# One 32 KB row per load, six buffers and two load queues in a row-wise infinity norm

## The chip, the cores and the metric

The kernel runs on one core of a Trainium2 chip. The metric is the device time of one execution in microseconds (us). The kernel before took 629.88 us, the median of three runs (629.82 to 629.88).

## The reference

The input `x` is 8192 rows by 8192 columns of float32, 268.4 MB. The output is one number per row, the largest absolute value of that row (`np.linalg.norm(x, ord=np.inf, axis=1)`), 32 KB in all. Every element is read once, and one reduction is done on it.

## The kernel before

A row of `x` is 32 KB. The 8192 rows are spread over 128 partitions, so that each partition reduces 64 rows; "row" below means one such step, 128 rows of `x`, one in each partition, 4 MB. The 64 rows form two stages.

**Bulk**, rows 0 to 47 (line 65 to 72). Each load (line 68) brings two neighbouring rows into each partition, 64 KB per partition and 8 MB in all, and one VectorE instruction (line 63, called through `absmax` at line 69) reduces both to two numbers in `r_bulk`. There are 24 such loads. Within a block of eight rows per partition the addresses of a partition are contiguous.

**Tail**, rows 48 to 63 (line 75 to 98). A buffer still holds two rows, but each row is loaded and reduced in the pieces that the list `TAIL` names (line 17 to 22): eight rows whole (8192 columns), five rows in halves of 4096, two in quarters of 2048, and the last as 2048, 2048, 2048, 1024, 512, 512. A piece's maximum goes into a cell of `part`, and one reduction of `part` gives `r_tail` for rows 48 to 62. The last row's first five maxima are put right behind that row's data in its own buffer, so that its last piece and those five numbers are reduced together, over 517 columns, into `r_fin`.

Buffers: the pool `sbuf` has three of 64 KB per partition (line 51). A load into a buffer waits until the reduction that read it three buffers earlier has ended; apart from that, and from a wait for the landing of the load that used the same completion semaphore before (there are eight in turn), loads are issued as fast as the queue takes them.

Queues: all loads of `x` go through one queue, SyncE's (SP below), in the order in which they are written. `r_bulk` is stored through ScalarE's queue (ACT, line 73) after the last bulk reduction, `r_tail` through the same (line 88), `r_fin` through SP at the end (line 99). VectorE does all reductions, in the order of the rows. ScalarE and GpSimd do no arithmetic on the data.

Of the kernel before, what the change touches and what calls it, by code (L numbers as in the profile page):

```python
# [1 line left out]
logging.getLogger("concourse").setLevel(logging.ERROR)  # L3

# [1 line left out]

# [4 lines left out]

F32 = mybir.dt.float32
X = mybir.AxisListType.X

TAIL = (
    [[8192]] * 8
    + [[4096, 4096]] * 5
    + [[2048] * 4] * 2  # L20
    + [[2048, 2048, 2048, 1024, 512, 512]]
)


@with_exitstack
def kernel(
    ctx: ExitStack,
    tc: tile.TileContext,
    x: bass.AP,
    out: bass.AP,  # L30
    G: int = 4,
    B: int = 2,
    BUFS: int = 3,
):
    nc = tc.nc
    P = nc.NUM_PARTITIONS
    rows, cols = x.shape


    n_tail = len(TAIL)  # L40
    assert n_tail % B == 0
    n_bulk_rows = rows // P - n_tail
    assert n_bulk_rows % (G * B) == 0
    A = n_bulk_rows // (G * B)
    split = n_bulk_rows * P
    x_b = x[:split].rearrange("(a p n b) c -> a n p (b c)", p=P, a=A, n=G, b=B)
    out_b = out[:split].rearrange("(a p n b) -> p a (n b)", p=P, a=A, n=G, b=B)
    x_t = x[split:].rearrange("(p t b) c -> t p (b c)", p=P, b=B)
    out_t = out[split:].rearrange("(p t) -> p t", p=P)

    sbuf = ctx.enter_context(tc.tile_pool(name="sbuf", bufs=BUFS))
    outp = ctx.enter_context(tc.tile_pool(name="outp", bufs=1))

    k_last = len(TAIL[-1])
    r_bulk = outp.tile([P, A, G * B], F32)
    r_tail = outp.tile([P, n_tail], F32)
    r_fin = outp.tile([P, 1], F32)
    k_max = max(len(r) for r in TAIL[:-1])
    part = outp.tile([P, n_tail - 1, k_max], F32)
    nc.vector.memset(part[:], 0.0)  # L60

    def absmax(o, i):
        nc.vector.reduce_max(out=o, in_=i, axis=X, apply_absolute_value=True)  # L63

    for a in range(A):
        for n in range(G):
            t = sbuf.tile([P, B * cols + 16], F32, tag="t")
            nc.sync.dma_start(out=t[:, : B * cols], in_=x_b[a, n])  # L68
            absmax(
                r_bulk[:, a, n * B : (n + 1) * B],  # L70
                t[:, : B * cols].rearrange("p (b c) -> p b c", b=B),
            )
    nc.scalar.dma_start(out=out_b, in_=r_bulk[:])

    for i in range(0, n_tail, B):
        t = sbuf.tile([P, B * cols + 16], F32, tag="t")
        for j in range(B):
            r = i + j
            at = j * cols
            last = r == n_tail - 1  # L80
            for k, w in enumerate(TAIL[r]):
                nc.sync.dma_start(  # L82
                    out=t[:, at : at + w], in_=x_t[i // B][:, at : at + w]
                )
                if last and k == k_last - 1:

                    absmax(r_tail[:, : n_tail - 1], part[:])
                    nc.scalar.dma_start(
                        out=out_t[:, : n_tail - 1], in_=r_tail[:, : n_tail - 1]
                    )  # L90
                    absmax(r_fin[:], t[:, at : B * cols + k_last - 1])
                elif last:
                    absmax(
                        t[:, B * cols + k : B * cols + k + 1], t[:, at : at + w]
                    )
                else:
                    absmax(part[:, r, k : k + 1], t[:, at : at + w])
                at += w
    nc.sync.dma_start(out=out_t[:, n_tail - 1 :], in_=r_fin[:])


# [1 line left out]
_INS = ['x']  # L103
_OUTS = [((8192,), 'float32')]


# [23 lines left out]
```

## Time and profile before

| what | value |
|---|---|
| median of three runs | 629.88 us |
| the profiled execution's own time | 629.88 us |
| its span, first to last instruction | 628.1 us |
| VectorE (DVE) busy | 552.7 us, 88% |
| bytes read from HBM | 268.44 MB, 427 GB/s over the span |
| loads of two rows / of one row / of 4096, 2048, 1024, 512 columns | 24 / 8 / 10, 11, 1, 2 |
| median us from issue to landing, whole rows of the tail | 37.0 |
| `r_bulk` store, 24 KB, from issue to landing | 57.9 us |

The profile comes from one execution taken by the hardware profiler. Its span is 1.78 us shorter than that execution's time; what lies around the span is not in the trace. The profiled execution took just the median of the runs. The line of DMA busy tenths shows, for each of 40 slices of the span, how busy the core's 16 DMA engines were on average. In a timeline, "x9" after an instruction means that nine instructions of that engine followed one another without a gap and are shown merged under the first one's name; "idle before <-" says how long the engine stood still ahead of it and what ended that.

### The profile page before, as it was taken

What the parts mean: (1) busy time and instruction counts of PE and PEld (TensorE: products, weight loads), DVE (VectorE), ACT (ScalarE), POOL (GpSimd) and SP (SyncE); (2) the same over time, 40 slices, a digit from 0 to 9 for tenths busy, and PEclk for the clock granted to TensorE, in tenths of its full rate; (3) what the DMA queues carried; (4) which work ended last, traced back from release to release, by engine and by line L of the source; (5) the groups of instructions that cost most, each with busy time, mean ns of one, the idle gap of its engine ahead of it and who ended that gap; (6) DMA issues with size and microseconds to landing.
All of it is one profiled execution on the core that took longest, in us unless ns stands there. A gap on an engine that the chain in (4) does not pass through costs nothing.

```text
span 628.1 us, 196 instructions
## 1 busy us (share of the span) xinstructions
DVE 552.7 (88%) x58; POOL 0.2 (0%) x4
## 2 busy tenths in 40 slices
DVE  0588988889988889888898888998889999999998
POOL 0000000000000000000000000000000000000000
DMA  9999999999999999999999999999999999999996
GB/s 401 413 455 413 455 413 455 413 455 413 455 413 455 409 459 413 455 413 455 413 455 413 455 413 455 413 455 413 455 405 430 434 435 432 420 432 432 424 426 274
DMA packets 9138, 268.49 MB, mean 427 GB/s; under 512 B 1968, under 2 KB 1968, under 8 KB 2352
## 3 DMA queue, kind: packets, MB, share of 16 engines
q1 hardware_dynamic: 8208, 268.44, 99.1%
q10 hardware_dynamic: 928, 0.03, 0.1%
q14 instruction: 2, 0.02, 0.0%
HBM read 268.44 MB, written 0.03 MB: 427 GB/s over the span
## 4 chain that ended last, share of the span: by engine, by line
DMA 64%; DVE 30%; another core or an unknown queue 4%; issue 1%; SPq 0%
DMA t<-in_x_dram 64%; DVE r_bulk L63 23%; DVE part L63 5%; DVE t L63 1%; SPq L82 0%; DVE r_fin L63 0%; SPq L68 0%
## 5 line engine op out<-in xcount | busy, mean ns | idle before, releaser
L63 DVE TENSOR_REDUCE r_bulk<-t 128x2 f32<-128x16384 f32 x24 | 413.3, 17219 | 70.5 <-DMA t<-in_x_dram 70.5
L63 DVE TENSOR_REDUCE part<-t 128x1 f32<-128x4096 f32 (+2 forms) x26 | 130.0, 5067 | 1.3 <-DMA t<-in_x_dram 1.3
L63 DVE TENSOR_REDUCE t<-t 128x1 f32<-128x2048 f32 (+2 forms) x5 | 8.6, 1746 | 0.4 <-DMA t<-in_x_dram 0.4
L60 DVE MEMSET part<- 128x60 f32 x1 | 0.1, 108 | 0.8 <-PEq L114 0.8
L63 DVE TENSOR_REDUCE r_fin<-t 128x1 f32<-128x517 f32 x1 | 0.7, 692 | 0.0
L63 DVE TENSOR_REDUCE r_tail<-part 128x15 f32<-128x60 f32 x1 | 0.2, 216 | 0.0
L114 POOL MEMSET const-bfloat16-1.0<- 128x1 bf16 x1 | 0.1, 101 | 0.0
L114 POOL MEMSET const-uint8-127<- 128x1 uint8 x1 | 0.1, 101 | 0.0
L114 POOL MEMSET const-float32-0.0<- 128x1 f32 x1 | 0.1, 98 | 0.2 <-issue 0.2
L114 POOL MEMSET const-float32-1.0<- 128x1 f32 x1 | 0.1, 98 | 0.0
## 6 DMA issues: line engine op xcount, KB each, us to landing
t<-in_x_dram SPq DMA_DIRECT2D x8, 4096.0 KB, 37.0
t<-in_x_dram SPq DMA_DIRECT2D x10, 2048.0 KB, 30.4
t<-in_x_dram SPq DMA_DIRECT2D x11, 1024.0 KB, 24.6
t<-in_x_dram SPq DMA_DIRECT2D x1, 512.0 KB, 15.9
t<-in_x_dram SPq DMA_DIRECT2D x2, 256.0 KB, 13.2
t<-in_x_dram SPq DMA_DIRECT2D x24, 40.7
out_dram<-r_bulk ACTq DMA_DIRECT2D x1, 24.0 KB, 57.9
out_dram<-r_tail ACTq DMA_DIRECT2D x1, 7.5 KB, 5.6
```

Of the source, the lines that this page charges most:

```text
L60: nc.vector.memset(part[:], 0.0)
L63: nc.vector.reduce_max(out=o, in_=i, axis=X, apply_absolute_value=True)
L114: nc = _bacc.Bacc("TRN2", target_bir_lowering=False, num_devices=1)
```

## The change

Loads of the bulk bring one row each: 48 loads of 32 KB per partition take the place of 24 of 64 KB, and 48 reductions over 8192 columns that of 24 over 16384. The pool has six buffers of one row each in place of three of two rows, so it holds the same bytes. A tail row too has a buffer of its own. The loads, bulk and tail counted through, go in turn to SP's and ACT's queue. The `r_bulk` store moves from ACT's queue to GpSimd's (POOL) and is written into the program near the end. `TAIL`, and so the sizes of all pieces, is unchanged. In the compiled order of VectorE the reduction of `part` into `r_tail` stood ahead of the last row's pieces; now it stands between the last row's fifth piece and `r_fin`.

```diff
-    B: int = 2,
-    BUFS: int = 3,
+    G: int = 8,
+    BUFS: int = 6,
...
-    x_b = x[:split].rearrange("(a p n b) c -> a n p (b c)", p=P, a=A, n=G, b=B)
+    x_b = x[:split].rearrange("(a p n) c -> a n p c", p=P, a=A, n=G)
...
-    x_t = x[split:].rearrange("(p t b) c -> t p (b c)", p=P, b=B)
+    x_t = x[split:].rearrange("(p t) c -> t p c", p=P)
...
+    queues = (nc.sync, nc.scalar)
+    n_loads = 0
+
+    def load(o, i):
+        nonlocal n_loads
+        queues[n_loads % 2].dma_start(out=o, in_=i)
+        n_loads += 1
+
     for a in range(A):
         for n in range(G):
-            t = sbuf.tile([P, B * cols + 16], F32, tag="t")
-            nc.sync.dma_start(out=t[:, : B * cols], in_=x_b[a, n])
-            absmax(
-                r_bulk[:, a, n * B : (n + 1) * B],
-                t[:, : B * cols].rearrange("p (b c) -> p b c", b=B),
-            )
-    nc.scalar.dma_start(out=out_b, in_=r_bulk[:])
+            t = sbuf.tile([P, cols + 16], F32, tag="t")
+            load(t[:, :cols], x_b[a, n])
+            absmax(r_bulk[:, a, n : n + 1], t[:, :cols])
 
-    for i in range(0, n_tail, B):
-        t = sbuf.tile([P, B * cols + 16], F32, tag="t")
-        for j in range(B):
...
+    for r in range(n_tail):
+        t = sbuf.tile([P, cols + 16], F32, tag="t")
+        at = 0
+        last = r == n_tail - 1
+        for k, w in enumerate(TAIL[r]):
+            load(t[:, at : at + w], x_t[r][:, at : at + w])
+            if last and k == k_last - 1:
+
+                absmax(r_tail[:, : n_tail - 1], part[:])
+                nc.gpsimd.dma_start(out=out_b, in_=r_bulk[:])
+                nc.scalar.dma_start(
+                    out=out_t[:, : n_tail - 1], in_=r_tail[:, : n_tail - 1]
                 )
...
+                absmax(r_fin[:], t[:, at : cols + k_last - 1])
+            elif last:
+                absmax(t[:, cols + k : cols + k + 1], t[:, at : at + w])
+            else:
+                absmax(part[:, r, k : k + 1], t[:, at : at + w])
+            at += w
     nc.sync.dma_start(out=out_t[:, n_tail - 1 :], in_=r_fin[:])
```

## The prediction

> **What bounds the kernel now.** I read the page's rows of busy time and DMA first, then the groups by shape, then stretches of the DMA rate, and last VectorE's timeline from 440 us on.
>
> ```profile
> DVE 552.7 (88%) x58; POOL 0.2 (0%) x4
> DMA  9999999999999999999999999999999999999996
> q1 hardware_dynamic: 8208, 268.44, 99.1%
> out_dram<-r_bulk ACTq DMA_DIRECT2D x1, 24.0 KB, 57.9
> ```
>
> The DMA engines are busy in every slice: loading bounds the kernel. VectorE is not far behind: 552.7 of 628.1 us. The next lines give a stretch, its length, VectorE's busy time in it and (last two columns) the DMA share and GB/s.
>
> ```profile
> 100.00:440.00 340.00, 303.90 (x18) 0.00 (x0) 1.00 1.00 434
> 470.00:484.00 14.00, 14.00 (x1) 0.00 (x0) 1.00 1.01 433
> 519.40:542.70 23.30, 23.30 (x3) 0.00 (x0) 1.00 1.00 428
> ```
>
> The third stretch is one in which, by the list of waits, SP's queue stood 23.2 us on the `r_bulk` store's landing. The DMA share is 1.00 there too: loads issued earlier covered it. So no stretch holds a DMA pause that more buffers or a second queue could close.
>
> VectorE's timeline (start, length, instruction, idle before):
>
> ```profile
> 448.11 17.22 DVE L63 TENSOR_REDUCE r_bulk<-t 128x2 f32<-128x16384 f32 x1 [2.06 <-DMA t<-in_x_dram]
> 467.49 17.22 DVE L63 TENSOR_REDUCE r_bulk<-t 128x2 f32<-128x16384 f32 x1 [2.15 <-DMA t<-in_x_dram]
> 484.62 60.23 DVE L63 TENSOR_REDUCE part<-t 128x1 f32<-128x8192 f32 x7
> 545.24 43.37 DVE L63 TENSOR_REDUCE part<-t 128x1 f32<-128x8192 f32 x9 [0.38 <-DMA t<-in_x_dram]
> ...
> 593.97 21.96 DVE L63 TENSOR_REDUCE part<-t 128x1 f32<-128x4096 f32 x9 [0.38 <-DMA t<-in_x_dram]
> ...
> 621.01 4.01 DVE L63 TENSOR_REDUCE t<-t 128x1 f32<-128x2048 f32 x3 [0.20 <-DMA t<-in_x_dram]
> 625.05 0.69 DVE L63 TENSOR_REDUCE r_fin<-t 128x1 f32<-128x517 f32 x1
> ```
>
> This is the view that decides. The last load of two rows lands at 467.5, and VectorE gets both at once. Though rows come singly from then on, it works without a pause until 544.85: seven more rows pass before it has caught up, since a row takes it (60.23 - 8.68) / 6 = 8.59 us (8.68 is the mean of that group) and a load about 9.7. From 545.24 it follows the loads closely, and ends 625.74. So what arrives late or in lumps near the end is regained slowly.
>
> **The change part by part.** The sum is made against the profiled execution, 629.88 us, which is the median too; its 1.78 us outside the span I leave.
>
> *Two queues.* What does an engine do with two queues that both hold loads? The `r_bulk` store on ACT's queue beside loads on SP's shows it. Its 24 KB are 768 runs of 32 bytes (128 partitions by six blocks), 48 per DMA engine, and 57.9 / 48 = 1.21 us each: just the time of one 32 KB run of a load on one engine (9.7 us / 8 partitions per engine). The trace's packet records agree: on an engine 32-byte packets lie between neighbouring 32 KB packets, one or a few at each gap, so queues take turns run by run. Two loads of equal runs, one on each queue and started together, then go at half speed each and land together, one run (1.2 us) apart, every 2 x 9.7 us. Nothing pulls them apart: a buffer comes free 8.6 or 17.2 us after a landing of the pair and four rows are still queued or in flight, two per queue, so neither queue runs dry. VectorE needs 17.2 us per 19.4 us pair, so the bulk hides this. The tail does not.
>
> The rows are an even number, so rows 54 and 55 (the last whole ones) form the last full pair. Row 55 lands when it does now, at 545.24 plus s, the cost of smaller runs; row 54 lands 1.2 us before it, instead of some 9.7. From row 54's landing VectorE has: two rows, 2 x 8.59 = 17.2; ten halves at (43.37 - 8.59 - 4.41) / 7 = 4.34, 43.4; eight quarters at (21.96 - 4.34 - 2.28) / 7 = 2.19, 17.5; the last row, 2 x 2.19 + 4.01 = 8.4; `r_tail`, 0.13 (616.09 - 615.96) and `r_fin` with its gap, 0.7. Together 87.3 us. Does it ever stand still in that time? Its lag behind landings is 16 us at first (17.2 - 1.2); a pair of halves takes it 8.7 us against 9.7 of loading, a pair of quarters 4.4 against 4.9. The last row's first pair starts at 545.2 + 17.2 + 43.4 + 17.5 = 623.3 and lands about 620. It never waits: 3 us stay in hand. VectorE, not the last load, sets the end.
>
> *32 KB runs for 64 KB in the bulk (s).* Bulk starts run from 42.11 to 448.11 over 21 loads: 19.333 us, 9.667 per row. Tail rows: (545.24 - 467.49) / 8 = 9.719. The difference, 0.052 x 48 rows = 2.5 us, is an upper bound, because the store's packets lie in the tail's figure; the lower is 0 (the rates 434 and 433 hardly differ). I take s = 1.2, the middle.
>
> So `r_fin` ends at 545.24 + 1.2 - 1.2 + 87.3 = 632.5 against 625.74: +6.8 us.
>
> *48 reductions for 24.* 2 x 8.59 for 17.14 (484.62 - 467.49): nothing, and covered by 2 us of idle time per load while loads bound. *More instructions on two queues.* An issue takes 0.33 us on SP, 0.35 to 0.44 on ACT; ACT issues nothing else in the bulk, and loads are issued at least a row ahead. Nothing, unless queued loads run out. *Six buffers.* The same bytes; they remove no pause, since there is none.
>
> *`r_tail` beside `r_fin`.* Its store took 5.6 us to land, among loads; `r_fin`'s took 1.4, with none. Now it is issued 0.7 us ahead of `r_fin`'s end with loads done: between 0 and 5.6 - 0.7 - 1.4 = 3.5 us. I take 0.1, since the loads that slowed it are gone.
>
> *`r_bulk` store on POOL.* POOL waits only for row 47's reduction and has nothing queued behind the store but the end. If it too goes run by run, with two loads' runs ahead of each of its 48, it needs at most 48 x 2.4 = 116 us from some 485 us, and less once runs are halved: done by 601, 30 us before the end. Ends: 0, and, if it lands last, 1 to 4 us (from `r_fin`'s 1.4 us to `r_tail`'s 5.6 after a 1.4 that is there anyway). I take 0.
>
> Sum: 629.88 + 6.8 + 0.1 = 636.8 us.
>
> A rule against my main step: the Trainium skill, "DMA: Bandwidth & Descriptors", section on queues, rings and completion order, says that an engine drains a packet of some 9 to 17 descriptors from one queue before it turns to the next. A whole load's share of an engine (eight runs and a mark) would then go in one turn, loads would land one after another, and the sum would be the first rival's. The records of single 32-byte packets between 32 KB ones speak for the row.
>
> A rule against the POOL store: "SBUF — State Buffer", section on the two sides, says that GpSimd-issued descriptors cannot be written while VectorE runs an instruction in a two-port mode. No POOL store is in this trace. By the rule the store could only start when VectorE ends; by the bounds above that is up to 640.8. But these reductions take 8.59 us for 8192 columns, about one element per ns, which does not look like a doubled mode.
>
> **The rivals.**
>
> *Loads land in turn* (queues alternate by loads, or the ACT queue starts half a pair late and stays so). For: ACT's first issue is not in this trace. Against: the packet records; and both queues wait for the same barrier at the start. Then the tail goes as now, plus s, plus at most 1.5 us of half-fitting lags: 630 to 633, say 631.8.
>
> *Two streams cost bandwidth.* For: 428 to 429 GB/s beside the store against 433. One per cent on the 545 us up to row 55 is 5.4 us on top: 642. Against: those were 32-byte packets, which equal runs are not.
>
> *Two queues speed the loads up, and it ends faster.* The place is the gap between packets on an engine. To repay 6.9 us the loads up to row 55 must be 6.9 / 543 = 1.3% faster, 440 GB/s; under 629.88 only beyond that, and at 442 GB/s about 627. Against: packets follow one another without a gap (DMA share 1.00 at 434), and no stretch shown exceeds 434.
>
> **How the numbers follow.** Pairs land together: 0.74, 634.5 to 640.8 by s and the stores, 636.8. In turn: 0.14, of which 0.04 within 0.2% (about 1.3 us, what a measurement of this kernel can tell from no change). Bandwidth lost: 0.08. Faster: 0.04. So slower 0.92, same 0.04, faster 0.04. The range reaches from 631.5, which takes in the better part of the second case, to 641; outside stay most of the bandwidth case, the fast case and the within-0.2% part, under 0.2.
>
> **What would show it.** Landings in pairs: in the bulk, VectorE's idle time of about 2 us before every second reduction and none before the others, and a median time from issue to landing for whole rows of some 41 to 50 us (a load issued 8.6 or 17.2 us after a landing lands with the third pair after it, 58 us after). No idle time on VectorE from about 545 us on; the last data some 7 us ahead of `r_fin`'s end; the rate still 432 to 434. The chain of waits should end in a long piece of VectorE. Idle time of 1 us before each single reduction would show landings in turn and prove the main step wrong; a rate above 438 or under 430 in the bulk would prove the cost of transfers wrong; a POOL store landing after `r_fin` would prove the last part wrong.

## The result and the profile after

The changed kernel takes 638.88 us (median of four runs, 638.73 to 638.96) against 629.88: 1.0141 times as long, 95% interval 1.0123 to 1.0158. The forecast was 636.8 us, slower, with a range of 631.5 to 641.0. The profiled execution took 638.96 us at a span of 637.2, so 1.8 us lie outside the span, as before.

From the page after, the rows that answer to those shown of before:

```profile
DVE 553.7 (87%) x82; POOL 1.1 (0%) x5
DMA  9999999999999999999999999999999999999992
q1 hardware_dynamic: 5904, 134.48, 49.3%
q10 hardware_dynamic: 5904, 133.97, 48.9%
t<-in_x_dram ACTq DMA_DIRECT2D x28, 4096.0 KB, 41.1
t<-in_x_dram SPq DMA_DIRECT2D x28, 4096.0 KB, 49.5
```

The two queues carry half of the bytes each, the DMA engines are as busy as before, and VectorE does the same work. Only the last digit of the DMA line has changed, from 6 to 2: the last slice is nearly without loads, since VectorE still works when they are done. The two rows of issues show whole rows landing 41 and 50 us after their issue (medians); the whole rows of the tail took 37 before.

VectorE's timeline of the changed kernel, in the bulk and at the end:

```profile
430.71 17.28 DVE L61 TENSOR_REDUCE r_bulk<-t 128x1 f32<-128x8192 f32 x2 [2.16 <-DMA t<-in_x_dram]
450.16 17.28 DVE L61 TENSOR_REDUCE r_bulk<-t 128x1 f32<-128x8192 f32 x2 [2.17 <-DMA t<-in_x_dram]
469.55 17.28 DVE L61 TENSOR_REDUCE r_bulk<-t 128x1 f32<-128x8192 f32 x2 [2.11 <-DMA t<-in_x_dram]
489.05 17.28 DVE L61 TENSOR_REDUCE part<-t 128x1 f32<-128x8192 f32 x2 [2.22 <-DMA t<-in_x_dram]
508.83 17.28 DVE L61 TENSOR_REDUCE part<-t 128x1 f32<-128x8192 f32 x2 [2.50 <-DMA t<-in_x_dram]
528.22 17.28 DVE L61 TENSOR_REDUCE part<-t 128x1 f32<-128x8192 f32 x2 [2.11 <-DMA t<-in_x_dram]
547.65 78.08 DVE L61 TENSOR_REDUCE part<-t 128x1 f32<-128x8192 f32 x20 [2.15 <-DMA t<-in_x_dram]
625.65 8.38 DVE L61 TENSOR_REDUCE t<-t 128x1 f32<-128x2048 f32 x5
633.95 0.20 DVE L61 TENSOR_REDUCE r_tail<-part 128x15 f32<-128x60 f32 x1
634.07 0.69 DVE L61 TENSOR_REDUCE r_fin<-t 128x1 f32<-128x517 f32 x1
```

Rows come in pairs: two reductions without a gap, then 2.1 us of idle time, again and again. The pairs go on past 484 us, where the kernel before had its rows singly and VectorE was catching up. The last full pair, rows 54 and 55, starts at 547.65, and from there VectorE does not stop until 634.76. Three stretches of the end show the loads stopping some 8 us before it (columns as before: stretch, length, busy time, then DMA share and GB/s last):

```profile
620.00:623.00 3.00, 3.00 (x2) 0.00 (x0) 1.00 1.03 423
623.00:626.00 3.00, 3.00 (x3) 0.00 (x0) 1.00 0.70 269
626.00:629.00 3.00, 3.00 (x2) 0.00 (x0) 1.00 0.00 0
```

So the 9.08 us (638.96 - 629.88) divide as follows. The packet records put the end of the last load's data at 626.03 against 623.22: 2.8 us for slower transfers. `r_fin` starts 8.04 us after that data (634.07) where it started 1.83 us after it (625.05): 6.2 us for VectorE's lag behind the loads. After `r_fin` there is 0.1 us more. These two numbers, the end of the data and the lag, are what the experiments are compared by.

### The profile page after: what moved, and what is told of

The parts are those of the page before. It is cut to its first block, busy times and chain, and to the rows that moved or that the text cites. A ratio compares the mean times of both kernels' runs of the same rounds, so it can differ in the third digit from the quotient of the medians.

```text
span 637.2 us, 285 instructions
## 1 busy us (share of the span) xinstructions
DVE 553.7 (87%) x82; POOL 1.1 (0%) x5
## 4 chain that ended last, share of the span: by engine, by line
DMA 73%; DVE 25%; issue 1%; DVEq 0%
DMA t<-in_x_dram 73%; DVE part L61 13%; DVE r_bulk L61 11%; DVE t L61 1%; DVE r_fin L61 0%; DVE r_tail L61 0%; DVEq L61 0%
## 5 line engine op out<-in xcount | busy, mean ns | idle before, releaser
L61 DVE TENSOR_REDUCE r_bulk<-t 128x1 f32<-128x8192 f32 x48 | 414.7, 8681 | 71.2 <-DMA t<-in_x_dram 71.2
```

## The experiments

Every kernel stands beside runs of the kernel before on the same chip; ratios are to those. "Data end" is the end of the last packet of `x` by the packet records, "lag" the time from it to the start of `r_fin`, both from the profiled execution. "Pairing theory" in the expectations is the prediction's main step: two rows land together, and VectorE works off that lump only slowly.

| kernel | median us | ratio, 95% interval | data end | lag |
|---|---|---|---|---|
| before | 629.88 | | 623.22 | 1.83 |
| changed | 638.88 | 1.0141 (1.0123 to 1.0158) | 626.03 | 8.04 |
| one queue throughout | 632.32 | 1.0039 (1.0025 to 1.0052) | 625.56 | 1.94 |
| two queues, tail on one | 632.58 | 1.0040 (1.0025 to 1.0055) | 625.87 | 1.95 |
| two queues, row 1 in three transfers | 653.68 | 1.0376 (1.0355 to 1.0398) | 640.50 | 7.03 |
| two queues, ACT's started some 6 us late | 635.58 | 1.0086 (1.0071 to 1.0102) | 626.37 | 4.53 |
| bulk on one queue, tail on two | 643.51 | 1.0214 (1.0196 to 1.0231) | 625.58 | 13.13 |
| halves of rows, one on each queue | 639.58 | 1.0151 (1.0138 to 1.0165) | 629.57 | 5.22 |
| halves of rows, one queue | 636.30 | 1.0101 (1.0084 to 1.0118) | 629.48 | 1.95 |

**One queue throughout.**

```diff
-    queues = (nc.sync, nc.scalar)
+    queues = (nc.sync, nc.sync)
```

> The changed kernel with every load on SP's queue; all else as changed (one row per load, six buffers, r_bulk store on POOL). Pairing theory: loads land singly, VectorE's idle time of about 1 us stands before each row, the tail goes as in the kernel before, and only the slower transfers of 32 KB runs remain: 631 to 632.7 us, I say 631.7. Rival (the cost is in the run size, the six one-row buffers or the moved stores, not in the second queue): 638 to 639. The pitch of a pair of rows in the bulk also tells what part of the 2.4 us by which row 55 came later is the run size (pitch then 19.43 as in the changed kernel) and what part is the second queue (pitch then nearer 19.33).

Measured: 632.32 us. Its timeline, first rows and last whole row:

```profile
12.99 8.69 DVE L61 TENSOR_REDUCE r_bulk<-t 128x1 f32<-128x8192 f32 x1 [12.05 <-DMA t<-in_x_dram]
22.68 8.69 DVE L61 TENSOR_REDUCE r_bulk<-t 128x1 f32<-128x8192 f32 x1 [1.01 <-DMA t<-in_x_dram]
32.40 8.69 DVE L61 TENSOR_REDUCE r_bulk<-t 128x1 f32<-128x8192 f32 x1 [1.03 <-DMA t<-in_x_dram]
...
547.27 43.48 DVE L61 TENSOR_REDUCE part<-t 128x1 f32<-128x8192 f32 x9 [1.04 <-DMA t<-in_x_dram]
...
627.50 0.69 DVE L61 TENSOR_REDUCE r_fin<-t 128x1 f32<-128x517 f32 x1
```

Single rows, 1.0 us of idle time before each, and the lag is 1.94 us again. So the second queue makes the lag; neither the six buffers nor the moved stores do. Rows take (547.27 - 12.99) / 55 = 9.714 us each, against 9.667 in the bulk of the kernel before and (547.65 - 22.93) / 54 = 9.717 in the changed one: so nearly all of the slower transfers comes with the loads of one row in runs of 32 KB, not with the second queue. Of the 2.8 us by which the data ends later in the changed kernel, 2.3 are there with one queue.

**Two queues in the bulk, the tail on one.**

```diff
-            load(t[:, at : at + w], x_t[r][:, at : at + w])
+            nc.sync.dma_start(out=t[:, at : at + w], in_=x_t[r][:, at : at + w])
```

> The changed kernel with alternating queues in the bulk, and all tail loads on SP's queue. Pairing theory: rows 46 and 47 are the last pair, VectorE has eight whole rows to catch up as after the last two-row load of the kernel before, so pairs in the bulk cost nothing but the transfers' 2 us: 632.3 us (631 to 633.5). Rival (two queues cost all through the bulk, or the one-row buffers do): 637 or more.

Measured: 632.58 us. The end of the pairs and what follows:

```profile
469.39 17.28 DVE L61 TENSOR_REDUCE r_bulk<-t 128x1 f32<-128x8192 f32 x2 [2.12 <-DMA t<-in_x_dram]
486.59 60.23 DVE L61 TENSOR_REDUCE part<-t 128x1 f32<-128x8192 f32 x7
547.59 43.47 DVE L61 TENSOR_REDUCE part<-t 128x1 f32<-128x8192 f32 x9 [0.77 <-DMA t<-in_x_dram]
...
627.82 0.69 DVE L61 TENSOR_REDUCE r_fin<-t 128x1 f32<-128x517 f32 x1
```

This is the pattern of the kernel before, shifted by 2 us: seven rows without a pause absorb the last pair, and row 55 is met at its landing. Pairs in the bulk cost nothing that shows; pairs in the tail cost the lag of 6.2 us.

**Bulk on one queue, tail on two.**

```diff
-            load(t[:, :cols], x_b[a, n])
+            nc.sync.dma_start(out=t[:, :cols], in_=x_b[a, n])
```

> The changed kernel with all bulk loads on SP's queue and only the tail's loads alternating. Taking turns run by run: ACT's row 49 is issued as soon as a buffer is free, when SP still has four rows ahead of row 48, so ACT's rows land well ahead of their turn while SP's go at half speed, VectorE waits for SP's rows, and pairs land about 14 us apart from each other to the end, out of order: 645.9 us (642 to 649), slower than two queues throughout. Rival (the loss is a matter of bandwidth with two queues): between the one-queue kernel and the changed one, 632 to 639.

Measured: 643.51 us, slower than two queues throughout, and 2.4 us less than worked out. What the first tail load on ACT's queue does to the rows that are due before it:

```profile
440.19 8.69 DVE L61 TENSOR_REDUCE r_bulk<-t 128x1 f32<-128x8192 f32 x1 [1.03 <-DMA t<-in_x_dram]
457.19 8.69 DVE L61 TENSOR_REDUCE r_bulk<-t 128x1 f32<-128x8192 f32 x1 [8.31 <-DMA t<-in_x_dram]
469.27 8.69 DVE L61 TENSOR_REDUCE r_bulk<-t 128x1 f32<-128x8192 f32 x1 [3.40 <-DMA t<-in_x_dram]
488.72 8.69 DVE L61 TENSOR_REDUCE r_bulk<-t 128x1 f32<-128x8192 f32 x1 [10.76 <-DMA t<-in_x_dram]
...
t<-in_x_dram ACTq DMA_DIRECT2D x4, 4096.0 KB, 23.4
```

VectorE waits up to 10.8 us for a row of SP's, while ACT's queue takes every second run for rows that nobody needs yet: its four whole rows land 23.4 us after their issue (median, last line, from the list of DMA issues), and row 49, issued at 439.2 us, is there at 462.5, ahead of rows 46 and 47 at 469.3 and 488.7. The data ends as with one queue (625.58), so no bandwidth is lost; the lag of 13.1 us is all order. A loss of bandwidth alone, as the rival had it, would have left this kernel between 632 and 639.

**ACT's queue half a load behind: first try.**

```diff
-            load(t[:, :cols], x_b[a, n])
+            if a == 0 and n == 1:
+                h, m = P // 2, cols // 2
+                nc.scalar.dma_start(out=t[:h, :cols], in_=x_b[a, n][:h])
+                nc.scalar.dma_start(out=t[h:, :m], in_=x_b[a, n][h:, :m])
+                nc.scalar.dma_start(out=t[h:, m:cols], in_=x_b[a, n][h:, m:])
+                n_loads += 1
+            else:
+                load(t[:, :cols], x_b[a, n])
```

> The changed kernel, but row 1, the first on ACT's queue, is loaded by three transfers that give each DMA engine twelve runs in place of eight: partitions 0 to 63 whole (four runs of 32 KB), partitions 64 to 127 in two halves of their columns (four and four runs of 16 KB). Both queues stay in use to the end. Pairing theory: queues take turns run by run, so ACT's loads stay four runs, half a load, behind SP's for good; landings in the bulk and the tail come one by one about 9.7 us apart, and the end comes some 5 us earlier than in the changed kernel: 634.2 us (633 to 635.5). Rival (two queues cost in themselves, wherever their loads stand to each other): no change, 638 to 639.

Measured: 653.68 us (ratio 1.0376, 1.0355 to 1.0398), and still pairs. The experiment missed its aim, and its trace shows two things. While the loads over 64 partitions ran, all transfers were slow:

```profile
2.00:40.00 38.00, 8.69 (x1) 0.00 (x0) 1.00 1.00 283
100.00:440.00 340.00, 301.57 (x36) 0.00 (x0) 1.00 1.00 432
```

That is 283 GB/s until 40 us; the data ends at 640.50, 14 us later than in the changed kernel. And the three transfers put no distance between the queues. One DMA engine's packets from the packet records, queue after the slash, KB and ns:

```
32/SP:1964  32/SP:1232  32/SP:1213  32/ACT:2008  32/SP:2227  32/ACT:2138  32/SP:2119  32/ACT:2127 ...
```

SP's queue was three runs ahead when ACT's began, and the twelve runs of ACT's row 1 after that end with SP's sixteenth, the last of its second row, to within a run: in step again, but now rows 1 and 2 are a pair, and at the end rows 53 and 54, which land 0.2 us apart (552.50 and 552.69). The lag of 7.03 us says nothing on the distance, but it does say what this other pairing of rows is worth by itself: 1.0 of the 8.04 us. The Trainium skill, "SBUF — State Buffer", section on door 1, says that partitions 0 to 63, or 64 to 127, reach half of the DMA ports. The packets here, some 2 us where others take 1.2, fit that.

**ACT's queue half a load behind: second try.**

```diff
+    idle = outp.tile([P, 1024], F32)
+    nc.vector.memset(idle[:], 0.0)
+    for _ in range(5):
+        late = nc.scalar.copy(out=idle[:], in_=idle[:])
...
-            load(t[:, :cols], x_b[a, n])
+            if a == 0 and n in (1, 3, 5):
+                with tc.issue_after(late.ins):
+                    load(t[:, :cols], x_b[a, n])
+            else:
+                load(t[:, :cols], x_b[a, n])
```

> The changed kernel with five copies of a small scratch tile (128 x 1024) on ScalarE ahead of its first load, so that ACT's queue starts some 6 to 8 us after SP's; the copies touch no data of the result. SP's loads run alone in that time and come to stand about half a load ahead. Pairing theory: turns taken run by run keep that distance for good, landings in the bulk are some 7 and 12 us apart in turn in place of 0.2 and 19.2, and the same two queues then cost less: 634.2 to 636.5 us. Rival (the distance closes up again, or two queues cost in themselves): 638 to 639.

Measured: 635.58 us, 3.3 less than the changed kernel with the same two queues and 0.3 us later data. The start and the last whole rows:

```profile
16.39 8.69 DVE L61 TENSOR_REDUCE r_bulk<-t 128x1 f32<-128x8192 f32 x1 [14.39 <-DMA t<-in_x_dram]
29.98 17.28 DVE L61 TENSOR_REDUCE r_bulk<-t 128x1 f32<-128x8192 f32 x2 [4.90 <-DMA t<-in_x_dram]
...
535.88 86.68 DVE L61 TENSOR_REDUCE part<-t 128x1 f32<-128x8192 f32 x21 [2.14 <-DMA t<-in_x_dram]
...
630.90 0.68 DVE L61 TENSOR_REDUCE r_fin<-t 128x1 f32<-128x517 f32 x1
```

Landings in the bulk lie some 5.7 and 13.8 us apart in turn (49.58, 55.28, 69.31, 74.95, 88.75 by the completion records), where 7 and 12 were expected, and the distance keeps: rows 53 and 54 land 5.2 us apart, at 535.86 and 541.07. VectorE starts its last unbroken stretch at 535.88, a row earlier in the order than in the changed kernel, and the lag falls to 4.53 us. The first try has the same pairs, rows 53 and 54 at the end, but landing together, and a lag of 7.03: so 1.0 of the 3.5 us gained goes with which rows are a pair, and the other 2.5 with the distance between their landings. Only this one distance was tried; how the cost goes with it is not shown.

**Halves of rows, on two queues and on one.** Both load each whole row as two halves of 4096 columns; in the second kernel both entries of the queue list are SP's.

```diff
-    [[8192]] * 8
-    + [[4096, 4096]] * 5
+    [[4096, 4096]] * 13
...
-            load(t[:, :cols], x_b[a, n])
+            load(t[:, : cols // 2], x_b[a, n][:, : cols // 2])
+            load(t[:, cols // 2 : cols], x_b[a, n][:, cols // 2 :])
```

> The changed kernel with every row of the bulk, and the first eight of the tail, loaded as two halves of 4096 columns, one on each queue (the tail's halves are reduced one by one, as rows 56 to 60 are). A pair that lands together is then one row, not two. Pairing theory: the lump at the end of the whole rows is half as large, 8.7 us of VectorE work, and runs of 16 KB add about 0.6 us over 48 rows: between the one-queue kernel and the changed one, 636.6 us by stepping the turns (634.5 to 637.5). Rival (lumps do not matter, run size does): smaller runs make it slower than the changed kernel, 639.5 or more.

Measured: 639.58 us, as the rival said. But the lag is 5.22 us, down from 8.04, as the pairing theory has it for a lump of one row; what was misjudged is the data's end, 629.57 in place of some 626.6 (626.03 and 0.6 for smaller runs). Its last unbroken stretch and `r_fin`:

```profile
600.16 26.29 DVE L60 TENSOR_REDUCE part<-t 128x1 f32<-128x4096 f32 x10 [1.05 <-DMA t<-in_x_dram]
...
634.79 0.69 DVE L60 TENSOR_REDUCE r_fin<-t 128x1 f32<-128x517 f32 x1
```

The second kernel was run to tell what the later end came from.

> The kernel with all whole rows loaded as two halves of 4096 columns, but with every load on SP's queue. It divides the cost that was misjudged there, a row every 9.79 us in the bulk in place of 9.71. If 16 KB runs cost that in themselves, the pitch here is 9.79 again and the time 636 to 637 us (the last data as late, VectorE 2 us behind it in place of 5). If it is 16 KB runs taken in turn from two queues, the pitch is 9.73, as the halves in the tail of the kernel before show (4.87 us each), and the time 632.5 to 634 us.

Measured: 636.30 us. Two rows of its bulk and its end:

```profile
13.04 8.69 DVE L60 TENSOR_REDUCE r_bulk<-t 128x1 f32<-128x8192 f32 x1 [12.11 <-DMA t<-in_x_dram]
...
472.88 8.69 DVE L60 TENSOR_REDUCE r_bulk<-t 128x1 f32<-128x8192 f32 x1 [1.11 <-DMA t<-in_x_dram]
...
631.42 0.69 DVE L60 TENSOR_REDUCE r_fin<-t 128x1 f32<-128x517 f32 x1
```

(472.88 - 13.04) / 47 = 9.784 us per row with one queue. So the second queue has no part in it: a row takes 9.667, 9.714 and 9.784 us with loads in runs of 64, 32 and 16 KB. The loads themselves shrink with the runs (8, 4 and 2 MB), but the packet records put most of the cost on the runs: on one engine they start 2.414, 1.211 and 0.609 us apart (medians in the bulk, one queue), which is 9.66, 9.69 and 9.74 us for the same bytes. The lag is back at 1.95, and the 3.3 us between these two kernels are the landing in pairs, now of halves.

**The store on POOL, and a shorter last piece.** Both start from the kernel before; the second has both edits.

```diff
-    nc.scalar.dma_start(out=out_b, in_=r_bulk[:])
+    nc.gpsimd.dma_start(out=out_b, in_=r_bulk[:])
...
-    + [[2048, 2048, 2048, 1024, 512, 512]]
+    + [[2048, 1536, 1536, 1024, 1024, 512, 512]]
```

> The kernel before with nothing changed but the r_bulk store, issued on POOL's queue in place of ACT's. In the changed kernel that store went out as 16 packets of 1536 bytes where ACT's queue sends 768 of 32 bytes. Theory: the store was covered in both kernels, and what can be gained is the time of those 768 packets, at most some 0.4 us: 629.5 to 629.9 us. Rival (the POOL queue costs time of its own at the start or the end): 631 or more.

> The kernel before with the r_bulk store on POOL's queue and the last row in pieces of 2048, 1536, 1536, 1024, 1024, 512, 512 columns. VectorE's last three reductions ahead of r_fin ran without a pause because the third 2048-column piece landed 2.5 us ahead of the end; smaller pieces let it start them sooner: some 0.4 us earlier than with the store alone, 629.0 to 629.6 us. Rival (each piece more costs as much as it saves): as the store alone.

Measured: 629.93 us with the store alone (ratio 0.9998, 0.9990 to 1.0007), 629.48 with both (0.9993, 0.9984 to 1.0002). The store's queue makes no difference here that the interval shows. With the shorter pieces VectorE runs through to `r_fin` without the two waits it had:

```profile
616.00 8.44 DVE L63 TENSOR_REDUCE t<-t 128x1 f32<-128x2048 f32 x6
624.47 0.69 DVE L63 TENSOR_REDUCE r_fin<-t 128x1 f32<-128x518 f32 x1
```

`r_fin` starts at 624.47 in place of 624.98 with the store alone. That half a microsecond is what the times show too, but the interval takes in no change, so this is no proven gain.

## Why the prediction was right

The direction, the mechanism and three quarters of the size were right (6.9 of 9.0 us); 2.1 us were missed, in two terms of the sum that set the start of VectorE's last stretch. The stretch was to start at 545.2 and started at 547.65.

- *Queues take turns run by run, and loads land in pairs.* Right. The timeline after shows the pairs, and both runs that kept single landings in the tail (one queue, tail on one queue) lost the lag. The Trainium skill's rule ("DMA: Bandwidth & Descriptors", section on queues, rings and completion order) of some 9 to 17 descriptors per turn, given there as typical, does not describe this trace: on each engine, packets of the two queues alternate one by one.
- *One run, 1.2 us, between the landings of a pair.* Wrong, 1.0 us of the miss. The two completions lie 0.2 us apart (469.52 and 469.70 for rows 46 and 47, 547.63 and 547.82 for rows 54 and 55). The packet records of one engine say why:

```
... 32768 SP, 32768 ACT, 32768 SP, 32768 ACT, 4 SP, 4 ACT, 32768 SP ...
```

The 4-byte mark that reports a load's end takes a turn of its own, so SP's mark waits for ACT's last run. The prediction knew of the mark and gave it no turn.
- *Runs of 32 KB for 64 KB, s = 1.2 us between 0 and 2.5.* Mis-sized by 1.4 us: by the completion records row 55 landed at 547.82 in place of 545.21, 2.6 us later and a little beyond the upper bound. With one queue it landed at 547.24, 2.0 us later. Where the remaining 0.6 us with two queues comes from is open; 0.4 of it stand already at row 1, which landed at 23.07 and with one queue at 22.66. The figure for the tail's rows, 9.719 us, was right for the bulk too (9.714); taking the middle because the store's packets lay in it was a mistake. The two errors add up to the 2.4 us by which the stretch started late. Moving that store to POOL in the kernel before gained nothing that its interval shows.
- *VectorE's chain, 87.3 us without a stop.* Right: 634.76 - 547.65 = 87.1.
- *The stores.* Right at 0.1 us for `r_tail`, which landed in 1.4 us, as the loads were done. The POOL store landed 9.6 us after its issue, far from the bound of 116 us and from the end. The Trainium skill's rule ("SBUF — State Buffer", section on the two sides) is for VectorE's two-port modes, and the prediction priced it, with a doubt, for these reductions (up to 640.8). The same page, under "Who interferes with whom", says that on trn2 `tensor_reduce`, which these are, has no such mode and never contends, and the trace agrees: with the tail on one queue, VectorE was busy without a break from 469.39 to past 546, and the store, issued at 486.97, landed 7.6 us later.
- *Six buffers, more instructions.* Nothing, as said: with one queue the buffers and the 48 reductions are all there, and the lag is not.
- *The rivals.* Loads landing in turn were to give 631.8; with one queue, where they do, the kernel takes 632.3. Two queues cost no bandwidth that shows at runs of 32 KB (9.717 against 9.714 us per row), and gained none: the bulk's 432 GB/s are the same with one queue and with two.

## What to carry to other kernels

Here the loads of one queue already kept the DMA engines busy, and a second queue added no rate (432 GB/s with either); it only changed the order in which data lands, and with turns taken run by run two equal loads started together end together, 0.2 us apart. That is harmless while the consumer has time to spare in each pair and dear just before the end, where every lump is worked off at the small difference of the two rates (here 9.7 against 8.6 us per row): where that holds, keep the last loads on one queue, in the order of use. And count a tail in two numbers, the end of the data and the lag of the last consumer behind it, because an edit can move one and leave the other alone: with one queue the lag went and the later data stayed.

## What was not expected

- The mark at the end of a load takes a turn of its own between two queues, so a pair's completions lie 0.2 us apart, not one run (1.2 us).
- The size of a contiguous run still matters between 16 and 64 KB: 9.667, 9.714 and 9.784 us per 4 MB row with runs of 64, 32 and 16 KB, with the DMA engines shown as fully busy in all three. Over 48 rows, 2.3 us and 5.6 us.
- The same 24 KB store of 768 pieces of 32 bytes lands in 57.9 us from ACT's queue and in 8.0 us from POOL's in the same kernel. The packet records show 768 packets of 32 bytes in the first, and 16 of 1536 bytes from POOL in the changed kernel. As the store is not on the path to the end, it saved nothing that the interval shows (0.9998, 0.9990 to 1.0007).
